# Two weight lines of a pair of banks: highs of both, then lows of both, in a pinned order

## The chip, the cores and the metric

The kernel runs on one core of a Trainium2 chip. The metric is the time of one execution on the device, in microseconds (us); before the change the median of three runs is 1748.11 us (1747.93 to 1748.73).

The engines are named as in the profile: PE is TensorE's matmuls and PEld its weight loads, DVE is VectorE, ACT is ScalarE, POOL is GpSimd, SP is SyncE.

## What is computed

A trunk of two layers on 256 tokens of width 1024, all in float32. Layer 0 mixes tokens by a gated short convolution, layer 1 by windowed attention. After each comes a channel mixer, PEER, that looks up experts by product keys. All norms are RMS norms. Cut to what matters here:

```
gate_b, gate_c, h = split(x @ w_in, 3)          # 1024 -> 3 x 1024, layer 0
x = x + (gate_b * conv(gate_c * h)) @ w_out
...
q  = t @ w_q                                    # 1024 -> 2048
idx, g = top 16 experts of 16384 by the keys, for each of 8 heads
h  = einsum("cd,ced->ce", t, u_tab[idx])        # chosen rows of u
x  = x + einsum("ce,ced->cd", g * gelu(h), v_tab[idx])
```

The kernel does not gather the expert rows. It multiplies the tokens by all 16384 rows of u, and by all of v with gates that are zero where an expert was not chosen.

## The kernel before

**Lines and their halves.** Every weight matrix is cut into lines of 128 x 1024 float32 (512 KB). `split_tile` (L176 to L185) loads a line into `raw` (four buffers) on SyncE's queue. ScalarE rounds it to `hi` (three buffers, L183), VectorE subtracts to get `lo` (two buffers, L184). The activation `xn` holds, for each of 8 blocks of 128 inputs, 256 columns of high halves and beside them 256 of low halves. A product of a line is high weights by high and by low activations, and low weights by high activations.

**Two forms of a product.** `wide_product` (L248) gives a line a bank of 512 columns: 8 matmuls of `hi` by all 512 columns (high and low activations side by side), then 8 of `lo` by the first 256. `sum_of_parts` (L259) later copies the right half of both banks (ScalarE) and adds the left half (VectorE). `cols_product` (L220), the narrow form, sums everything in 256 columns, with 24 matmuls. Its order depends on its last argument; without one it is 8 of `lo`, then 16 of `hi`:

```
turns = [(lo, k, 0) for k in range(KC)] + [(hi, k, n) for k in range(KC) for n in range(2)]
```

**Which lines are wide.** In `conv_mixer` (loop at L471) each j takes three lines: two that share a pair of banks, wide for j = 1 to 6, and one for the gate, always narrow (L484). In `peer`, stage pq (L989) takes 16 lines two by two, all wide but the first two. Stage ph, over u, takes 128 lines in two halves of 64, two by two (L1106):

```
wide = (j % 4 == 2 or j >= HALF // 2) if half == 0 else j < HALF - 2
```

So wide and narrow pairs alternate in the first 32 lines, and the last pair of all is narrow. Stage pv, over v, has products of 512 columns of another kind (`rows_product`), which the change leaves alone.

**Order of the work.** `take()` (L208) first brings the queue of split lines to two, then takes the first; so the line after the one in hand is split while that one is multiplied. A new `lo` waits until the matmuls of the line two before have read theirs. Which instruction stands where in its engine's queue is settled at compile time by a scheduler that follows program order and the readiness that it reckons with; an edge (`tc.issue_after(ins)`) keeps an instruction behind another on its engine. `bg.pump()` (L56) is called between products and hands out pieces of background work, mostly VectorE's: top 16 of the scores, gates, one-hot tables (L1025) and their small products pg on TensorE (L1040). Each piece is kept behind the latest `lo` on VectorE.

**Banks.** Wide pairs have two pairs of banks in turn (`two_banks`, L137), narrow products one bank each.

Of the kernel before, what the change touches and what calls it, by code (L numbers as in the profile page):

```python
# [18 lines left out]
T = 256  # L19
D = 1024  # L20
NT = T // P
KC = D // P
# [53 lines left out]
def trunk_kernel(  # L76
# [29 lines left out]
    bg = Background(tc)  # L106

    newest = []

    def matmul(*a, **k):  # L110
        newest[:] = [PE.matmul(*a, **k).ins]  # L111
        return newest[0]
# [5 lines left out]
    def in_turn():  # L118

        return tc.issue_after(newest[0])  # L120
# [11 lines left out]
    def bank(tag, name):  # L132
        if tag == "acc":
            return four_banks(False).tile([P, 512], F32, tag=tag, name=name, bufs=4)
        return ps.tile([P, 512], F32, tag=tag, name=name, bufs=2)
# [40 lines left out]
    def split_tile(src, spare=False, pieces=1):  # L176
        raw = strm.tile([P, D], F32, tag="raw", name="raw", bufs=4)
        hi = strm.tile([P, D], F32R, tag="hi", name="hi", bufs=3)
        lo = strm.tile([P, D], F32R, tag="oh2" if spare else "lo", name="lo", bufs=2)
        n = D // pieces  # L180
        for c in (slice(n * i, n * i + n) for i in range(pieces)):
            nc.sync.dma_start(raw[:, c], src[:, c])
            bg.rounded = S.copy(hi[:, c], raw[:, c]).ins  # L183
            bg.behind = V.tensor_tensor(lo[:, c], raw[:, c], hi[:, c].bitcast(F32), ALU.subtract).ins  # L184
        return hi, lo  # L185
# [22 lines left out]
    def take(n=2):  # L208

        prefetch(n)  # L210
        return ahead.popleft()

    def prefetch(n, spare=False, pieces=1):
        while order and len(ahead) < n:
            with ExitStack() as held:
                for ins in evicted:
                    held.enter_context(tc.issue_after(ins))
                ahead.append(split_tile(order.popleft(), spare, pieces))

    def cols_product(dst, w, act, nth=None):  # L220

        hi, lo = (a.rearrange("p (k c) -> p k c", k=KC) for a in w)
        if nth == 0:
            turns = [(w, k, n) for w, n in ((hi, 0), (lo, 0), (hi, 1)) for k in range(KC)]
        elif nth == 1:
            turns = [(w, k, n) for w, n in ((hi, 0), (hi, 1), (lo, 0)) for k in range(KC)]
        else:
            turns = [(lo, k, 0) for k in range(KC)] + [(hi, k, n) for k in range(KC) for n in range(2)]
        for i, (w, k, n) in enumerate(turns):
            matmul(dst, w[:, k], act[:, k, T * n : T * n + T], start=(i == 0), stop=(i == 3 * KC - 1))  # L230
# [14 lines left out]
        run([turn for k in range(4, KC) for turn in ((hi, k - 4, 1), (hi, k, 0), (lo, k, 0))])  # L245
        run([(hi, k, 1) for k in range(4, KC)], stop=True)

    def wide_product(b, w, act, between=None):  # L248

        hi, lo = (a.rearrange("p (k c) -> p k c", k=KC) for a in w)  # L250
        for k in range(KC):
            matmul(b, hi[:, k], act[:, k], start=(k == 0), stop=False)
        if between:
            with in_turn():
                between()
        for k in range(KC):
            matmul(b[:, :T], lo[:, k], act[:, k, :T], start=False, stop=(k == KC - 1))

    def sum_of_parts(dst, b):  # L259
        S.copy(dst, b[:, :, T:])  # L260
# [149 lines left out]
    def factors():  # L410

        b = bank("g", "pyb")
        for t in range(NT):
            transpose(b[:, P * t : P * t + P], stat[:, 8 + t : 9 + t].to_broadcast([P, P]), ident)
        S.copy(yb, b[:, :T])
# [29 lines left out]
    def conv_mixer(sc):  # L445
        cw = sc(KC, 3)
        xn = turned_x(0, big.tile([P, KC, 2 * T], F32R, tag="xa", name="xn"))
        wait_for(nc.gpsimd.dma_start(cw, conv_w).ins, [bg.rounded])
        loaded = load_buckets(sc)
        z = big.tile([P, KC, 2 * T], F32R, tag="HB", name="z")  # L450
        ring = [(sc(2, T), sc(T + 2), sc(T)) for _ in range(2)]
        for _, ch, _ in ring:
            V.memset(ch, 0.0)

        def mixed(j, b0, b1):
            cs, ch, y = ring[j % 2]
            if 0 < j < KC - 1:
                sum_of_parts(cs, b0)
                V.tensor_tensor(cs, cs, yb[:, None, :].to_broadcast([P, 2, T]), ALU.mult)
            else:  # L460
                times_factor(cs, b0, 2)
            V.tensor_tensor(ch[:, 1 : T + 1], cs[:, 0], cs[:, 1], ALU.mult)
            V.tensor_scalar(y, ch[:, 0:T], cw[:, j, 0:1], None, op0=ALU.mult)
            V.scalar_tensor_tensor(y, ch[:, 1 : T + 1], cw[:, j, 1:2], y, op0=ALU.mult, op1=ALU.add)
            V.scalar_tensor_tensor(y, ch[:, 2 : T + 2], cw[:, j, 2:3], y, op0=ALU.mult, op1=ALU.add)
            V.tensor_tensor(y, y, yb, ALU.mult)
            V.tensor_tensor(y, b1[:, :T], y, ALU.mult)
            S.copy(z[:, j, :T], y)
            V.tensor_tensor(z[:, j, T:], y, z[:, j, :T].bitcast(F32), ALU.subtract)

        for j in range(KC):  # L471
            if j == 2:
                bias_rows(*loaded)
                blank_table(1)
            wide = 0 < j < KC - 1
            b0, b1 = two_banks("pconv") if wide else bank("u", "pconv"), None
            for i in range(2):
                if wide:
                    between = (lambda: (factors(), mixed(*left))) if (j, i) == (1, 0) else None
                    wide_product(b0[:, i], take(), xn, between)  # L480
                else:
                    cols_product(b0[:, T * i : T * i + T], take(), xn, 3 * j + i)
            b1 = bank("g", "pgate")
            cols_product(b1[:, :T], take(), xn)  # L484
            if j == 0:
                left = j, b0, b1
            else:
                mixed(j, b0, b1)
        acc = accumulators("pout")
        for k in range(KC - 2):  # L490
            rows_product(acc, take(), z[:, k, :T], z[:, k, T:], k == 0)
        return last_rows(acc, [(take(KC - k), z[:, k, :T], z[:, k, T:]) for k in (KC - 2, KC - 1)])
# [250 lines left out]
    def peer(layer, last, meanwhile):  # L743
# [8 lines left out]
        xr = turned_x(1 + 2 * layer, big.tile([P, KC, 2 * T], F32R, tag="HA", name=f"xr{layer}"), last, bq[:, :T])  # L752
        xn = big.tile([P, KC, 2 * T], F32R, tag="xa", name="xn")
# [235 lines left out]
        for c in range(0, NSUB, 2):  # L989
            q = qT[(c // 4) % 2][:, c % 4 : c % 4 + 2]  # L990
            b = two_banks("pq") if c else bq
            for i in range(2):
                if c:
                    wide_product(b[:, i], take(), xr)
                elif i:
                    cols_product(b[:, T:], take(), xr, i)
                bg.pump()
            if c:
                sum_of_parts(q, b)
            else:  # L1000
                S.copy(q, b.rearrange("p (a t) -> p a t", a=2))
            if c == 2:
                factors()
            if c >= 4 and c % 4 == 0:
                compared(c - 4)
# [91 lines left out]
        for half, hm in enumerate(halves):  # L1097
            if half == 1:
                spread_half(0)
                bg.plan(bg.cost(), HALF - 4)  # L1100
            for j in range(0, HALF, 2):
                if half == 0 and j == HALF // 2:
                    bg.drain()
                    second_tile()
                    bg.plan(bg.cost(), HALF // 2 + 14)
                wide = (j % 4 == 2 or j >= HALF // 2) if half == 0 else j < HALF - 2  # L1106
                b = two_banks("ph") if wide else bank("u", "ph")
                for i in range(2):
                    if wide:
                        wide_product(b[:, i], take(), xn)  # L1110
                    else:
                        cols_product(b[:, T * i : T * i + T], take(), xn)
                    bg.pump()
                if wide:
                    sum_of_parts(hm[:, j : j + 2], b)
                    S.activation(hm[:, j : j + 2], hm[:, j : j + 2], AF.Gelu)  # L1116
                else:
                    S.activation(hm[:, j : j + 2], b.rearrange("p (a t) -> p a t", a=2), AF.Gelu)
                if half == 0 and j == 0:
                    first_picks()  # L1120
                if half == 1 and j >= HALF - 16 and j % 4 == 0:
                    far_pump()
# [70 lines left out]
        for j in range(0, P, 2):  # L1193
# [12 lines left out]
            a = aring[:, (j // 2) % 4]  # L1206
# [44 lines left out]
    total, part, root = stat[:, 4:6], stat[:, 6:8], stat[:, 8:10]  # L1251
# [34 lines left out]
    for n, (t, c) in enumerate(ends):  # L1286
        h = c.start // 512
        if c.start == 768:
            b = bank("u", "pend")[:, :T]
# [99 lines left out]
```

## Time and profile before

| | |
|---|---|
| median of three runs | 1748.11 us |
| the profiled execution | 1748.41 us |
| its span, first to last instruction | 1746.6 us |
| VectorE busy | 1358.3 us, 78% |
| ScalarE busy | 931.7 us, 53% |
| one rounding to `hi` (L183) | 1049 ns, 595 times |
| one subtraction to `lo` (L184) | 1221 ns, 595 times |
| moved by DMA | 375.51 MB, 215 GB/s on average |

The timeline lists start, duration, engine, line, operation and count, with successive instructions of one kind merged. Matmuls overlap: one of 512 columns lasts some 393 ns, and the next starts 227 ns after it; so the pace is read from starts. Line 111 is the helper through which every matmul goes, and tiles are told apart by name: pconv and pgate (convolution), pq, ph, pv and pg (PEER).

### The profile page before, as it was taken

How to read it: one execution, taken by the hardware profiler on the slowest of the kernel's cores; microseconds unless marked ns; L12 is line 12 of the kernel's file. 1: busy time of each engine (PE TensorE's matmuls, PEld its weight loads, DVE VectorE, ACT ScalarE, POOL GpSimd, SP SyncE). 2: the span in 40 equal slices, each digit the busy share in tenths (PEclk: the TensorE clock that was granted, in tenths of full speed). 3: DMA queues.
4: the chain of work that ended last, by engine and by line, in shares of the span. 5: the costliest groups of instructions: out<-in, count | busy, mean ns of one | idle time of the engine just before them, and what ended most of it. 6: DMA issues, size and time to landing. Idle time of an engine off the chain costs nothing.

```text
span 1746.6 us, 28965 instructions
## 1 busy us (share of the span) xinstructions
PE 1736.7 (99%) x10153; PEld 1503.1 (86%) x10153; DVE 1358.3 (78%) x2850; ACT 931.7 (53%) x1262; POOL 1026.2 (59%) x584
## 2 busy tenths in 40 slices
PE   9999999999999999999999999999999999999998
PEld 7989998888888888888888899888888888888886
DVE  7869989987777667666586899898877777666765
ACT  5455555565545444454476655655655544444544
POOL 1112888888888886530010148888888888865100
PEclk9999999999999999999999999999999999999999
DMA  7987777776679898998685867777766798988884
GB/s 258 313 279 222 185 182 192 188 187 182 169 177 238 220 221 235 272 267 242 213 274 171 285 176 190 183 192 187 189 176 174 190 234 221 222 239 232 245 241 136
DMA packets 255698, 375.51 MB, mean 215 GB/s; under 512 B 135765, under 2 KB 170613, under 8 KB 255296
## 3 DMA queue, kind: packets, MB, share of 16 engines
q1 hardware_dynamic: 86976, 314.35, 55.9%
q0 software_dynamic: 82112, 30.69, 16.3%
q10 hardware_dynamic: 86464, 28.62, 6.7%
q8 instruction: 79, 1.29, 0.3%
q14 instruction: 67, 0.55, 0.1%
HBM read 344.96 MB, written 28.61 MB: 214 GB/s over the span
## 4 chain that ended last, share of the span: by engine, by line
PE 98%; DVE 1%; ACT 0%; issue 0%; DVEq 0%; ACTq 0%
PE ph L111 41%; PE pv L111 40%; PE pq L111 6%; PE pconv L111 3%; PE pgate L111 1%; PE psc L111 1%; PE pwo L111 1%; PE pg L111 1%; PE pout L111 1%; PE po L111 0%; PE ppt L115 0%; PE pk L111 0%; DVE xs L300 0%; PE ptr L115 0%; PE pwarm L111 0%; ACT xn L344 0%
## 5 line engine op out<-in xcount | busy, mean ns | idle before, releaser
L183 ACT CAST hi<-raw 128x1024 fp32r<-128x1024 f32 (+1 forms) x597 | 625.2, 1048 | 588.4 <-PE pv L111 192.8
L184 DVE TENSOR_TENSOR lo<-raw,hi 128x1024 fp32r<-128x1024 f32 (+1 forms) x597 | 726.1, 1219 | 271.6 <-ACT hi L183 152.0
L539 POOL DMA_INDIRECT table<-route x256 | 473.5, 1850 | 129.6 <-issue 74.4
L111 PE MATMUL ph<-xn,hi 128*128 128x512 f32 (+1 forms) x2336 | 515.3, 366 | 0.1
L111 PE MATMUL pv<-hi,xn 128*128 128x512 f32 (+1 forms) x2048 | 507.9, 389 | 0.0
L111 PEld LDWEIGHTS pv<-hi,xn 128*128 128x128 f32 x2048 | 384.2, 188 | 79.7
L539 POOL DMA_INDIRECT far_table<-yb x192 | 366.4, 1908 | 119.0 <-DMA far_table<-yb 59.8
L111 PEld LDWEIGHTS ph<-xn,hi 128*128 128x128 f32 x2336 | 387.0, 190 | 56.9 <-DVE route L261 0.2
L111 PEld LDWEIGHTS ph<-xn,lo 128*128 128x128 f32 x2048 | 275.8, 191 | 17.4 <-DVE lo L184 0.4
L111 PE MATMUL ph<-xn,lo 128*128 128x256 f32 x2048 | 283.5, 282 | 0.0
L111 PE MATMUL pv<-lo,xn 128*128 128x512 f32 x1024 | 277.0, 390 | 0.0
L111 PEld LDWEIGHTS pv<-lo,xn 128*128 128x128 f32 x1024 | 191.5, 188 | 39.3 <-DVE lo L184 0.3
L539 POOL DMA_INDIRECT set_table<-yb x64 | 134.7, 2104 | 19.5 <-issue 19.2
L1162 POOL DMA_DIRECT2D far_gates<-far_table x28 | 15.3, 546 | 150.6 <-DVE route L1175 126.5
L527 POOL DMA_DIRECT2D table<-blank x16 | 18.6, 1165 | 138.8 <-DMA table<-blank 96.1
L1181 ACT CAST xn<-hm 128x512 fp32r<-128x512 f32 x64 | 39.9, 623 | 74.9 <-PE pv L111 73.8
L1182 DVE TENSOR_TENSOR xn<-hm,xn 128x512 fp32r<-128x512 f32 x64 | 44.2, 691 | 35.8 <-ACT xn L1181 27.8
L111 PE MATMUL pq<-xr,hi 128*128 128x512 f32 (+1 forms) x288 | 68.2, 374 | 0.2
L1181 ACT CAST xn<-route 128x512 fp32r<-128x512 f32 x64 | 39.7, 620 | 46.8 <-PE pv L111 45.7
L1182 DVE TENSOR_TENSOR xn<-route,xn 128x512 fp32r<-128x512 f32 x64 | 44.0, 688 | 24.3 <-ACT xn L1181 23.7
L111 PEld LDWEIGHTS pq<-xr,hi 128*128 128x128 f32 x288 | 49.5, 189 | 8.9 <-ACT xr L344 0.8
L1116 ACT ACTIVATE route<-route 128x512 f32<-128x512 f32 x62 | 39.0, 629 | 15.2 <-DVE oh L1036 7.8
(216 smaller groups left out, 1478.9 us busy)
## 6 DMA issues: line engine op xcount, KB each, us to landing
raw<-in_u SPq DMA_DIRECT2D x256, 512.0 KB
raw<-in_v SPq DMA_DIRECT2D x256, 512.0 KB
table<-blank POOLq DMA_DIRECT2D x16, 1024.0 KB
raw<-in_w_q SPq DMA_DIRECT2D x32, 512.0 KB
gates<-table ACTq DMA_DIRECT2D x128, 128.0 KB
raw<-in_w_in SPq DMA_DIRECT2D x23, 512.0 KB
far_table<-blank POOLq DMA_DIRECT2D x6, 1024.0 KB
raw<-in_w_qk SPq DMA_DIRECT2D x10, 512.0 KB
```

What stands on the lines that cost most here:

```text
L111: newest[:] = [PE.matmul(*a, **k).ins]
L183: bg.rounded = S.copy(hi[:, c], raw[:, c]).ins
L184: bg.behind = V.tensor_tensor(lo[:, c], raw[:, c], hi[:, c].bitcast(F32), ALU.subtract).ins
L527: ins = nc.gpsimd.dma_start(dst, blank[:, None, :].to_broadcast([P, ROWS // P, P])).ins
L539: nc.gpsimd.indirect_dma_start(to, bass.IndirectOffsetOnAxis(ap=places[:, c : c + 1], axis=0), gates[:, c : c + 1], None, compute_op=ALU.a ...
L1116: S.activation(hm[:, j : j + 2], hm[:, j : j + 2], AF.Gelu)
L1162: ins = (nc.gpsimd if i == 2 else nc.scalar).dma_start(f[:, i], part).ins
L1181: copied[:] = [S.copy(a[:, 0], src).ins]
L1182: return V.tensor_tensor(a[:, 1], src, a[:, 0].bitcast(F32), ALU.subtract).ins
```

## The change

`wide_product` becomes `wide_pair`, which takes both lines of a pair first and multiplies high of the first, high of the second, low of the first, low of the second. Background work is handed out after the second part and after the last. The split of the next line is asked for after the first line's lows, that of the line behind it after the second line's. Each matmul of these pairs, and the narrow products of conv_mixer, pq and ph as groups, are kept behind the one before by an edge, so the order of products on TensorE is that of the program.

```diff
-    def wide_product(b, w, act, between=None):
-
-        hi, lo = (a.rearrange("p (k c) -> p k c", k=KC) for a in w)
-        for k in range(KC):
-            matmul(b, hi[:, k], act[:, k], start=(k == 0), stop=False)
+    chain = []
+
+    def after_chain():
+        return tc.issue_after(chain[0]) if chain else ExitStack()
+
+    def narrow(dst, act, nth=None):
+        with after_chain():
+            cols_product(dst, take(), act, nth)
+        chain[:] = newest
+
+    def wide_pair(b, act, between=None):
+
+        pair = [[a.rearrange("p (k c) -> p k c", k=KC) for a in take(2 - i)] for i in range(2)]
+
+        def part(i, low):
+            for k in range(KC):
+                with after_chain():
+                    chain[:] = [
+                        matmul(b[:, i, :T], pair[i][1][:, k], act[:, k, :T], start=False, stop=(k == KC - 1))
+                        if low else matmul(b[:, i], pair[i][0][:, k], act[:, k], start=(k == 0), stop=False)
+                    ]
+
+        part(0, False)
         if between:
             with in_turn():
                 between()
-        for k in range(KC):
-            matmul(b[:, :T], lo[:, k], act[:, k, :T], start=False, stop=(k == KC - 1))
+        part(1, False)
+        bg.pump()
+        part(0, True)
+        prefetch(1)
+        part(1, True)
+        prefetch(2)
+        bg.pump()
...
-            for i in range(2):
-                if wide:
-                    between = (lambda: (factors(), mixed(*left))) if (j, i) == (1, 0) else None
-                    wide_product(b0[:, i], take(), xn, between)
-                else:
-                    cols_product(b0[:, T * i : T * i + T], take(), xn, 3 * j + i)
+            if wide:
+                wide_pair(b0, xn, (lambda: (factors(), mixed(*left))) if j == 1 else None)
+            else:
+                for i in range(2):
+                    narrow(b0[:, T * i : T * i + T], xn, 3 * j + i)
             b1 = bank("g", "pgate")
-            cols_product(b1[:, :T], take(), xn)
+            narrow(b1[:, :T], xn)
...
-                for i in range(2):
-                    if wide:
-                        wide_product(b[:, i], take(), xn)
-                    else:
-                        cols_product(b[:, T * i : T * i + T], take(), xn)
-                    bg.pump()
+                if wide:
+                    wide_pair(b, xn)
+                else:
+                    for i in range(2):
+                        narrow(b[:, T * i : T * i + T], xn)
+                        bg.pump()
```

The loop of pq is changed in the same way as that of ph.

More of the change, by code (lines that the diff above doesn't have):

```diff
@@ L991, in peer @@
             b = two_banks("pq") if c else bq
-            for i in range(2):
[L993 to L996, printed above, removed]
+            if c:
+                wide_pair(b, xr)
+            else:
+                bg.pump()
+                narrow(b[:, T:], xr, 1)
                 bg.pump()
@@ L1107, in peer @@
                 b = two_banks("ph") if wide else bank("u", "ph")
-                for i in range(2):
-                    if wide:
-                        wide_product(b[:, i], take(), xn)
-                    else:
-                        cols_product(b[:, T * i : T * i + T], take(), xn)
-                    bg.pump()
+                if wide:
+                    wide_pair(b, xn)
+                else:
+                    for i in range(2):
+                        narrow(b[:, T * i : T * i + T], xn)
+                        bg.pump()
                 if wide:
```

## The prediction

> **What bounds the kernel now.** I read the busy times of the page first, then the chain that ended last, then what the weight loads of TensorE wait for, then the groups by shape, and at last the timeline, in a quiet stretch and around one change of form.
>
> ```profile
> span 1746.6 us, 28965 instructions
> ...
> PE 1736.7 (99%) x10153; PEld 1503.1 (86%) x10153; DVE 1358.3 (78%) x2850; ACT 931.7 (53%) x1262; POOL 1026.2 (59%) x584
> ...
> PEclk9999999999999999999999999999999999999999
> ...
> PE 98%; DVE 1%; ACT 0%; issue 0%; DVEq 0%; ACTq 0%
> ```
>
> TensorE is busy for 99% of the span, holds 98% of the chain and has its clock throughout. Whatever TensorE waits is added to the time, and whatever other engines wait is not. The waits of the weight loads say how well the split of the weights keeps up:
>
> ```profile
> PEld ph L111 <- DVE lo L184: 0.4, 1, 0.4
> PEld pv L111 <- DVE lo L184: 0.3, 1, 0.3
> ```
>
> In 1746.6 us the loads waited twice for a low half from VectorE. So VectorE is not late today; the question is by how much.
>
> Now the shapes, with the columns line, engine, operation, tile, shape and count, then busy us and mean ns:
>
> ```profile
> L111 PE MATMUL ph<-xn,hi 128*128 128x512 f32 x1760 | 442.6, 393 | 0.1
> ...
> L111 PE MATMUL pq<-xr,hi 128*128 128x512 f32 x224 | 56.8, 395 | 0.0
> ...
> L111 PE MATMUL ph<-xn,hi 128*128 128x256 f32 x576 | 75.0, 283 | 0.0
> ...
> L111 PE MATMUL pconv<-xn,hi 128*128 128x512 f32 x96 | 24.3, 393 | 0.0
> ```
>
> A wide line has 8 high products of 512 columns, a narrow one 16 of 256. So there are 1760/16 = 110 wide pairs in ph, 224/16 = 14 in pq and 96/16 = 6 in pconv: 130 pairs. The 576 high products of 256 columns are 36 narrow lines of ph.
>
> **What the new order gains on TensorE.** Start times, not durations, give the pace, since the matmuls overlap. A quiet stretch of ph (start us, us, engine, line, operation, count):
>
> ```profile
> 350.08 1.12 PE L111 MATMUL ph<-xn,lo 128*128 128x256 f32 x8
> 351.03 2.00 PE L111 MATMUL ph<-xn,hi 128*128 128x512 f32 x8
> 352.87 1.11 PE L111 MATMUL ph<-xn,lo 128*128 128x256 f32 x8
> 353.82 2.00 PE L111 MATMUL ph<-xn,hi 128*128 128x512 f32 x8
> 355.66 1.12 PE L111 MATMUL ph<-xn,lo 128*128 128x256 f32 x8
> ```
>
> And a stretch of pv, where every product has 512 columns:
>
> ```profile
> 535.20 1.07 PE L111 MATMUL pv<-lo,xn 128*128 128x512 f32 x4
> 536.11 1.98 PE L111 MATMUL pv<-hi,xn 128*128 128x512 f32 x8
> 537.92 1.07 PE L111 MATMUL pv<-lo,xn 128*128 128x512 f32 x4
> ```
>
> In pv twelve products take 537.92 - 535.20 = 2.72 us, 0.227 each. In ph eight highs take 351.03 to 352.87, 1.84 us, where eight at the pace of pv would take 1.81: a run of 512 columns that follows one of 256 loses 0.03 us at its start. Eight lows take 0.95 us, and sixteen in a row (178.64 to 180.56 in the next fence) 1.92, so a run of lows gains 0.01 where it follows highs. One return trip from highs to lows and back costs 0.02 us. The change removes one trip of two from each of 130 pairs: 130 x 0.02 = 2.6 us gained. The bounds are nothing and twice that, since starts are given to 0.01 us and the difference is two such steps.
>
> The Trainium skill ("TensorE: Matmul & The Clock Gate", Back-to-back issue gap) gives the gap between matmuls by their columns alone, N / 2.4 + 2.5 ns, which leaves no cost to the change from 256 to 512 columns; by that the reordering itself would gain 0. The trace does not agree: the 512-column runs differ by 0.03 us with what stands before them.
>
> **What it costs: the low half of the next narrow line.** Low halves lie in two buffers. Today the first line's lows are multiplied before the second line's highs, so its buffer is free 2.79 us (351.03 to 353.82) before the pair ends. After the change both low buffers are held until the pair's last quarter. If a wide pair follows, that is no matter: it begins with highs, of which there are three buffers. A narrow line without its own order begins with its lows. The trace around such a change of form, a wide pair whose second line is followed by a narrow line:
>
> ```profile
> 175.85 1.12 PE L111 MATMUL ph<-xn,lo 128*128 128x256 f32 x8
> 176.80 2.00 PE L111 MATMUL ph<-xn,hi 128*128 128x512 f32 x8
> 178.64 2.08 PE L111 MATMUL ph<-xn,lo 128*128 128x256 f32 x16
> 180.56 2.08 PE L111 MATMUL ph<-xn,hi 128*128 128x256 f32 x16
> ```
>
> ```profile
> 177.06 1.22 DVE L184 TENSOR_TENSOR lo<-raw,hi 128x1024 fp32r<-128x1024 f32 x1 [0.30 <-issue]
> ```
>
> ```profile
> 180.44 1.99 PEld L111 LDWEIGHTS ph<-xn,hi 128*128 128x128 f32 x16
> ```
>
> The x16 of lows is the second line's eight and the narrow line's eight. The low half of the narrow line is written by the VectorE row: it starts at 177.06, 0.09 us after the first line's lows end (175.85 + 1.12 = 176.97), which is when their buffer comes free, and is ready at 178.28. Its first load comes eight lows after 178.64, near 179.5: a slack of some 1.2 us, all of it from the second line's highs that lie between.
>
> The change takes just those highs away from between. Count from the start of the first line's lows: VectorE starts at 177.06 - 175.85 = 1.21 and is done at 2.43. How long from there to the load is shown where TensorE did wait, at the first narrow line of ph behind pq:
>
> ```profile
> 153.75 1.22 DVE L184 TENSOR_TENSOR lo<-raw,hi 128x1024 fp32r<-128x1024 f32 x1
> ```
>
> ```profile
> 155.02 1.01 PEld L111 LDWEIGHTS ph<-xn,lo 128*128 128x128 f32 x8
> ```
>
> The load starts 155.02 - 154.97 = 0.05 us after the write ends. So the narrow line can start at 2.48. TensorE is there earlier: sixteen lows of the pair take 1.92 us, and a load goes 0.12 us ahead of its matmul (180.44 against 180.56), so it asks at 1.80. It waits 2.48 - 1.80 = 0.68 us, with nothing of the pinned chain to put in between: pinned, the narrow line's highs stand behind its lows.
>
> How often: the loops give it. In ph's first half lines 4, 8, ..., 28 are narrow and follow a wide pair (7), in the second half the last pair is narrow (1), and ph's first narrow line follows pq's last wide pair (1): 9 a layer, 18. In conv_mixer the gate's line follows the wide pair for j = 1 to 6: 6. Together 24 x 0.68 = 16.3 us. The second narrow line is not late: its low half is written right after, done at 2.43 + 1.22 = 3.65, and asked for a whole narrow line (24 products at 0.12 = 2.88) after 2.48.
>
> Bounds for one wait: nothing below 0.6 follows from these rows, as the write itself (1.22) outlasts the second line's lows (0.95). Upward it grows if VectorE is busy when the buffer comes free. The write at 153.75 is such a case today, since its load had to wait; but there VectorE will have 1.84 us more before the buffer is free, as long as the background steps keep their place, so I take 0.68 for all and put the rest into the range.
>
> **What moves at no cost.** Highs have three buffers and are wanted a full line earlier than lows; two of three stay as they are, and the third comes free earlier, after the pair's first highs. A load into raw is issued when a low half is done, today one every 2.79 us, afterwards two 1.22 us apart every 5.58 us. Of the waits of ScalarE's casts these stand side by side (us, times, longest):
>
> ```profile
> ACT hi L183 <- PE ph L111: 191.6, 147, 2.8
> ...
> ACT hi L183 <- DMA raw<-in_u: 20.6, 11, 3.4
> ```
>
> The cast waits for a buffer 147 times and for the transfer 11 times, and no load of ph waits for it, so four raw buffers cover the bunching; if they did not, a wide pair would be late by what the transfer lacks. SyncE's queue holds only such loads. VectorE's low halves for the next wide pair are ready at 2.43 and 3.65 on the same count and are wanted at 1.92 + 16 x 0.227 + 0.03 - 0.12 = 5.46 and 0.96 later: slacks of 2.98 and 2.77 us. The two background calls of a pair now both lie between the second low half and the next pair's first. The evacuation still follows the pair's last low, as the two banks were summed together before too.
>
> **The sum.** The profiled execution took 1748.41 us, 1.8 above its span and 0.3 above the median of 1748.11. 1748.4 + 16.3 - 2.6 = 1762.1, with the median's 0.3 off 1761.8: I say 1762.
>
> **The rivals.** *Grouping without the wait.* If the narrow line's lows were ready (a free buffer, or VectorE far ahead), only the gain is left: 1748.1 - 2.6 = 1745.5, faster. It needs fewer than 2.6 / 0.68 = 4 waits of the 24. Two buffers speak against it, and the 0.09 us between their release and the write. Chance 0.07.
>
> *The change does not do what it says*: TensorE follows the old order anyway, or the pair is broken up by other work. Then 1748, no change. The chain of products is explicit, so 0.05.
>
> *VectorE's blocks become the bound for wide pairs too.* In ph's second half the one-hot steps come in one block between two low halves:
>
> ```profile
> 449.51 1.23 DVE L184 TENSOR_TENSOR lo<-raw,hi 128x1024 fp32r<-128x1024 f32 x1 [0.91 <-PE ph L111]
> 450.65 0.69 DVE L1033 TENSOR_TENSOR oh<-iota,i1T 128x1024 bf16<-128x1024 bf16 x1
> ...
> 455.33 1.08 DVE L1038 TENSOR_TENSOR oh<-oh,gT 128x512 bf16<-128x512 bf16 x3
> 456.33 2.35 DVE L184 TENSOR_TENSOR lo<-raw,hi 128x1024 fp32r<-128x1024 f32 x2
> ```
>
> From 450.74 to 456.33 is 5.59 us. After the change the free gap between pairs of low halves is 5.58 - 2 x 1.22 = 3.14, so the block makes the next two 2.45 late, and of the slack of 2.77 for the second 0.3 is left. A block longer by 0.3, or one caught between the two low halves, stalls TensorE. There are 16 one-hot steps a layer, done two by two: 16 blocks in all. If each costs 0.7 us, that is 11 us more: 1773. It decides from the point where a block exceeds 5.9 us. Chance 0.18.
>
> *Only the wait, no gain*: each product costs what its own columns cost, whatever stands before it, and 1748.1 + 16.3 = 1764.4. The 0.03 us by which runs of highs differ speak against it: 0.06. It is what the formula of the Trainium skill cited above ("TensorE: Matmul & The Clock Gate", Back-to-back issue gap) would make of the change.
>
> **How the numbers follow.** The forecast, the wait less the gain, has 0.64: 1762, by itself 1757 to 1768 (half to twice the gain, and waits 0.3 us longer in a third of the places, or absent in a quarter). The range takes in the blocks and the case without gain, and reaches down to where half the waits are gone: 1753 to 1774. Left out are the faster case and no change, 0.12, and blocks dearer than 0.7 us. A measurement of this kernel can tell 0.2% (3.5 us) from no change. Slower by more: 0.64 + 0.18 + 0.06 = 0.88; within 0.2%: 0.05 for no change and 0.03 of the case without the wait, whose 2.6 us lie inside 0.2%, together 0.08; faster by more: the other 0.04 of that case, where the gain is nearer its upper bound.
>
> **What would show it.** Right: the waits of PEld have a new line for ph behind lo of L184 with about 18 entries of 0.6 to 0.8 us, and one for pgate with 6; the timeline has x16 highs of 512 columns and lows behind them; each VectorE write of a narrow line's low half starts 0.1 us after the pair's first lows end. The busy share of TensorE falls by about 1 in 100. Wrong: no such waits (then the buffer was free, and the time falls), or waits at wide pairs in ph's second half (then the blocks), or waits behind hi of L183 or a raw transfer, which none of the steps above has.

## The result and the profile after

| | before | after |
|---|---|---|
| median of five runs | 1748.04 us (1747.68 to 1748.73) | 1765.37 us (1764.84 to 1766.95) |
| the profiled execution | 1748.41 us | 1764.84 us |
| its span | 1746.6 us | 1763.1 us |

The ratio is 1.01, 95% interval 1.0088 to 1.0111: the change makes the kernel 17.3 us slower. The forecast was 1762, so it was short by 3.4 us, inside its range. In the three longer of the five runs after (1765.37 to 1766.95) the mean granted clock of TensorE is 0.998, in the other two (1764.84, which was profiled, and 1764.98) it is 0.999, as before the change.

The page of the kernel after, in the order in which it was read before: span, busy times, chain.

```profile
span 1763.1 us, 28971 instructions
...
PE 1739.3 (99%) x10153; PEld 1502.7 (85%) x10153; DVE 1349.3 (77%) x2850; ACT 941.1 (53%) x1262; POOL 1004.9 (57%) x584
...
PE 91%; DVE 5%; issue 2%; DMA 1%; ACT 1%; SPq 0%; ACTq 0%; DVEq 0%
```

The busy share of TensorE is 99% in both, and hides the loss twice. It is rounded: 1746.6 - 1736.7 = 9.9 us were idle before, 1763.1 - 1739.3 = 23.8 us are idle after. And matmuls overlap, so a late one leaves a gap that is shorter than its delay. The chain says it better: TensorE's share falls from 98% to 91%, and VectorE's rises to 5%. (5% of the span is 88 us, far more than was lost, since the chain runs on through whole VectorE steps whenever TensorE waits for one's end.) The waits of the weight loads (us, times, longest):

```profile
PEld ph L111 <- DVE lo L184: 13.4, 17, 2.3
...
PEld pgate L111 <- DVE lo L184: 3.5, 5, 1.0
...
PEld pgate L111 <- ACT mix L283: 1.0, 1, 1.0
```

Behind `lo` of L184 there was one entry of 0.4 for ph before; there are 17 now, and 5 for pgate. The entry put down to `mix` is the sixth gate: VectorE's write came after the mixing there too. The timeline around a change of form in ph, a wide pair followed by a narrow line (the convention is that of the prediction: start, duration, engine, line):

```profile
184.63 2.07 PE L111 MATMUL ph<-xn,lo 128*128 128x256 f32 x16
...
185.84 2.36 DVE L184 TENSOR_TENSOR lo<-raw,hi 128x1024 fp32r<-128x1024 f32 x2 [1.43 <-issue]
...
187.12 1.01 PEld L111 LDWEIGHTS ph<-xn,lo 128*128 128x128 f32 x8 [0.62 <-DVE lo L184]
187.12 1.22 PE L111 MATMUL ph<-xn,lo 128*128 128x256 f32 x8 [0.42 <-DVE lo L184]
```

The x16 is the pair's lows of both lines. VectorE starts 185.84 - 184.63 = 1.21 us after them, the narrow line's first load comes at 187.12, 2.49 after. Without a wait it would come at 1.80 (1.92 for sixteen lows less the lead of 0.12): 0.69 us lost. Three readings of one delay stand in these rows: 0.62 is idle time of the loads, counted from the end of the load before, which normally overlaps the next; 0.42 is the gap in the overlapping matmuls; 0.69 is what the end of the kernel sees. The entries of the waits add up so: 2.28 + 1.80 behind pq (below) and 15 of some 0.62 (0.56 to 0.68) make 13.4.

Where the time came from, by stage, each counted from its first weight load to that of the next, in us:

| stage | before | after | difference |
|---|---|---|---|
| start | 10.34 | 9.89 | -0.45 |
| pconv, pgate | 69.58 | 74.10 | +4.52 |
| pq, layer 0 | 51.88 | 54.52 | +2.64 |
| ph, layer 0 | 371.88 | 375.91 | +4.03 |
| pq, layer 1 | 51.79 | 54.05 | +2.26 |
| ph, layer 1 | 372.12 | 375.78 | +3.66 |
| all others | 819.03 | 818.80 | -0.23 |

All of the loss lies in the stages that have wide pairs. In pq the loss is at its end, where ph's first narrow line waits:

```profile
157.15 2.08 PE L111 MATMUL pq<-xr,lo 128*128 128x256 f32 x16
...
159.02 0.18 DVE L844 TENSOR_SCALAR route<-route 128x32 uint32<-128x32 uint32 x1
...
160.38 0.19 DVE L853 TENSOR_TENSOR route<-route 128x32 bf16<-128x32 f32 x1
160.50 2.35 DVE L184 TENSOR_TENSOR lo<-raw,hi 128x1024 fp32r<-128x1024 f32 x2
161.77 1.01 PEld L111 LDWEIGHTS ph<-xn,lo 128*128 128x128 f32 x8 [2.28 <-DVE lo L184]
```

The buffer is free 1.21 us after 157.15, at 158.36. VectorE writes into it only at 160.50: until then it works through routing steps that the background calls handed out ahead of the write. In layer 1 the same place waits 1.80. One of the two dear gates looks alike, with mixing steps in the place of routing:

```profile
51.46 2.07 PE L111 MATMUL pconv<-xn,lo 128*128 128x256 f32 x16
...
52.75 0.43 DVE L492 TENSOR_TENSOR z<-mix,z 128x256 fp32r<-128x256 f32 x1 [0.47 <-ACT z L491]
53.10 2.35 DVE L184 TENSOR_TENSOR lo<-raw,hi 128x1024 fp32r<-128x1024 f32 x2
54.37 1.01 PEld L111 LDWEIGHTS pgate<-xn,lo 128*128 128x128 f32 x8 [1.04 <-DVE lo L184]
```

The write starts 1.64 us after the lows instead of 1.21. By starts of matmuls, 0.1 us added for the slower second one, the six gates lose 1.04, 0.68, 0.73, 1.10, 0.62 and 0.62: 4.8 us together. The sum of all waits: 16 changes of form in ph, 14 at 0.68 (one of them 0.74) and two at 0.62 where a layer ends (10.8), two behind pq (2.36 + 1.88 = 4.2), six gates (4.8): 19.8 us, against 16.3 in the forecast.

### The profile page after: what moved, and what is told of

It reads as the page before. It is cut to its first block, busy times and chain, and to the rows that moved or that the text cites. A ratio compares the mean times of both kernels' runs of the same rounds, so it can differ in the third digit from the quotient of the medians.

```text
span 1763.1 us, 28971 instructions
## 1 busy us (share of the span) xinstructions
PE 1739.3 (99%) x10153; PEld 1502.7 (85%) x10153; DVE 1349.3 (77%) x2850; ACT 941.1 (53%) x1262; POOL 1004.9 (57%) x584
## 3 DMA queue, kind: packets, MB, share of 16 engines
q8 instruction: 79, 1.29, 0.3%
## 4 chain that ended last, share of the span: by engine, by line
PE 91%; DVE 5%; issue 2%; DMA 1%; ACT 1%; SPq 0%; ACTq 0%; DVEq 0%
PE pv L111 40%; PE ph L111 38%; PE pq L111 4%; DVE lo L184 2%; PE pconv L111 2%; PE pwo L111 1%; PE pout L111 1%; PE pg L111 1%; PE pgate L111 1%; PE psc L111 1%; ACT hi L183 1%; PE po L111 0%; DMA raw<-in_w_in 0%; PE ppt L115 0%; DMA raw<-in_w_q 0%
## 5 line engine op out<-in xcount | busy, mean ns | idle before, releaser
L184 DVE TENSOR_TENSOR lo<-raw,hi 128x1024 fp32r<-128x1024 f32 (+1 forms) x597 | 718.6, 1221 | 264.6 <-ACT hi L183 146.7
L561 POOL DMA_INDIRECT table<-route x256 | 455.1, 1778 | 135.7 <-issue 74.4
L111 PE MATMUL ph<-xn,hi 128*128 128x512 f32 (+1 forms) x2336 | 493.3, 364 | 0.1
L111 PEld LDWEIGHTS ph<-xn,hi 128*128 128x128 f32 x2336 | 394.1, 189 | 63.0 <-DVE route L284 0.3
L561 POOL DMA_INDIRECT far_table<-yb x192 | 378.3, 1970 | 114.3 <-DMA far_table<-yb 57.4
L111 PE MATMUL ph<-xn,lo 128*128 128x256 f32 x2048 | 271.6, 284 | 10.4 <-DVE lo L184 9.9
L111 PEld LDWEIGHTS ph<-xn,lo 128*128 128x128 f32 x2048 | 261.5, 191 | 21.6 <-DVE lo L184 13.4
L561 POOL DMA_INDIRECT set_table<-yb x64 | 119.8, 1872 | 24.1 <-issue 18.9
```

The costliest lines, as they stand in the source:

```text
L561: nc.gpsimd.indirect_dma_start(to, bass.IndirectOffsetOnAxis(ap=places[:, c : c + 1], axis=0), gates[:, c : c + 1], None, compute_op=ALU.a ...
```

## The experiments

Theory: narrow lines begin with lows, and their low half cannot be written before the pair's last quarter, since both low buffers are held; TensorE waits 0.68 us at 24 places, more where VectorE is busy, and the order of wide pairs itself gains some 0.02 us a pair. Rivals: the edges that pin the order cost the time; or the order of products inside wide pairs does, whatever follows them; or products cost by their columns alone, and nothing is gained. Every experiment is an edit of the kernel after unless said. "Before" in a result is the kernel before on the same chip.

**Narrow lines begin with highs** (e1), and the same edit made in the kernel before (e4).

```diff
-            cols_product(dst, take(), act, nth)
+            cols_product(dst, take(), act, 1 if nth is None else nth)
```

> The changed kernel, in which every narrow line of conv_mixer and ph that had its lows first now has its 16 highs first and its lows last. If the loss is the wait for the narrow line's low half (0.68 us, 24 times, more behind pq), sixteen highs at 0.12 us are 1.92 us of work ahead of the lows and cover it: the waits of PEld for lo of L184 in ph and pgate go, and the time falls below the old kernel's by the gain of the grouping, 1745 to 1746 us. If the loss is the pinned order by itself, or VectorE's load, it stays near 1765.

Measured: 1749.33 us, before 1747.95; ratio 1.0006 (0.9997 to 1.0015). Of the 17.3 us 16 are gone with the lows' turn alone, while highs of both lines still stand ahead of lows and the order is pinned. ph takes 371.61 and 371.55 us, 0.3 and 0.6 less than before. So the loss sits at the narrow lines, not in the wide pairs. The time expected was 1745 to 1746, below the kernel before by the gain of the grouping, and that was missed by 3 to 4 us: waits use the gain up. The largest lie in pconv, which takes 72.22, 2.6 more than before. From the trace of this kernel, in that stage:

```profile
66.20 1.22 DVE L184 TENSOR_TENSOR lo<-raw,hi 128x1024 fp32r<-128x1024 f32 x1
67.33 0.42 DVE L485 TENSOR_TENSOR mix<-mix 128x256 f32<-128x256 f32 x1
...
70.28 0.42 DVE L490 TENSOR_TENSOR mix<-pgate,mix 128x256 f32<-128x256 f32 x1
70.62 1.22 DVE L184 TENSOR_TENSOR lo<-raw,hi 128x1024 fp32r<-128x1024 f32 x1
...
71.89 1.00 PEld L111 LDWEIGHTS pgate<-xn,lo 128*128 128x128 f32 x8 [1.38 <-DVE lo L184]
```

Six mixing steps, from 67.33 to 70.70, stand between the pair's second low half and the gate's, which comes later than the gate's own highs can cover. Matmuls wait 1.34 us here and 0.26, 0.40 and 0.42 at three other places; with 0.1 each for the slower second product that is 2.8. In conv_mixer the mixing leaves VectorE too little room. Behind pq, in ph's first narrow line, the loads still wait 0.65 and 0.55 us for its low half, 1.3 with the slower second products. So 4.1 us of waits stand against a gain of 2.6 (the pairs of ph repeat every 5.567 us here too, see the account below). That is read from the trace; no run isolates it.

> The old kernel with only the narrow lines' order turned, highs first: the control for the same turn in the changed kernel. The old one has no waits there to win back, and the number of changes between 512 and 256 columns is the same, so both theories expect no change, 1747.5 to 1748.5 us. If it were faster by itself, that would have to be taken off what the turn does in the changed kernel. The difference to the changed kernel with highs first is the gain of the grouping alone, 2.6 us by the forecast (130 pairs at 0.02).

Measured: 1748.77 us, before 1747.95; 1.0004 (0.9995 to 1.0013). In the old order the turn of the narrow lines makes no difference. It matters only behind grouped pairs.

**Three highs first, then the lows** (e2): a dose between the two, 3 x 0.12 = 0.36 us of cover.

```diff
+        elif nth == 3.5:
+            turns = [(hi, k, 0) for k in range(3)] + [(lo, k, 0) for k in range(KC)]
+            turns += [(hi, k, 0) for k in range(3, KC)] + [(hi, k, 1) for k in range(KC)]
...
-            cols_product(dst, take(), act, nth)
+            cols_product(dst, take(), act, 3.5 if nth is None else nth)
```

> The changed kernel with three of the narrow line's highs (256 columns) ahead of its eight lows in conv_mixer and ph, the other thirteen behind. A dose: three highs are 0.36 us of the 0.68 us that the line waits for its lows. If the wait is what the buffer and VectorE's write make it, each of the 24 waits falls by 0.36 us: 1765.4 - 8.6 = 1756.8 us, with waits of 0.32 us left in ph. If the waits came from the order of VectorE's queue, they would move with it and the time stay near 1765.

Measured: 1758.18 us, before 1748.2; 1.0062 (1.0048 to 1.0076). The waits of this kernel's loads:

```profile
PEld ph L111 <- DVE lo L184: 7.1, 18, 1.9
PEld pgate L111 <- DVE lo L184: 3.0, 6, 0.9
```

Without the two behind pq (1.85 and 1.14) the 16 others have (7.1 - 3.0) / 16 = 0.26 of idle loads, where the kernel after has 0.62: the 0.36 of cover came off one for one. Of the 1.4 us above the expectation 0.7 lie at the gates (pconv is 72.68 us, 1.42 under the kernel after, where six times 0.36 would be 2.16) and 0.6 in the start (10.48).

**The pins alone, and the order alone.** e5 keeps the edges and puts the old order back; e3 keeps the order of the program and drops the edges.

```diff
         part(0, False)
...
-        part(1, False)
-        bg.pump()
         part(0, True)
+        bg.pump()
         prefetch(1)
+        part(1, False)
         part(1, True)
```

> The changed kernel with its pins, but each pair in the old order: high and low of the first line, then high and low of the second; the split of the next line is asked for after the first line's lows. If the loss is the buffer that the grouping holds longer, the waits go and the time is the old one's, 1747 to 1749 us. If pinning costs by itself, it stays above that, up to 1765.

Measured: 1748.89 us, before 1747.95; 1.0006 (0.9997 to 1.0015). Pinning the old order costs nothing that can be measured.

```diff
     def after_chain():
-        return tc.issue_after(chain[0]) if chain else ExitStack()
+        return ExitStack()
```

> The changed kernel without the edges that pin the order of products; all else as it is. The order that the scheduler then writes puts two or three highs of 512 columns of a later pair (0.227 us each) ahead of most narrow lines' lows. If the loss is the wait of 0.68 us, these fill 0.45 us of it some 20 times: 1765.4 - 9 = about 1756 us, with waits of 0.2 us left. If the grouping itself costs (more distance between highs and lows), it stays at 1765; if the pin is all of the loss, it comes to 1746 to 1748.

Measured: 1759.26 us, before 1747.95; 1.0066 (1.0053 to 1.008): 6.1 us under the kernel after by the medians, 3 over the expectation. A change of form in this kernel:

```profile
183.54 2.08 PE L111 MATMUL ph<-xn,lo 128*128 128x256 f32 x16
185.45 0.63 PE L111 MATMUL ph<-xn,hi 128*128 128x512 f32 x2
186.03 1.22 PE L111 MATMUL ph<-xn,lo 128*128 128x256 f32 x8
```

The narrow line's lows start 186.03 - 183.54 = 2.49 us after the pair's, to the hundredth as in the kernel after: the low half is no earlier. But two products of a later wide pair have been put ahead of them, and these fill 2 x 0.227 = 0.45 of the 0.68. The trace has such a pair at 14 places of ph, 6.3 us. So pins keep the scheduler from filling a wait that another part of the change makes. The expectation was too low for two reasons. Behind pq (loads idle for 1.80 and 2.10 us) and at the gates the scheduler filled little. And right after the second of these waits, which ends at 1026.01, the granted clock is 0.50 from 1027.5 to 1030.9 us: products of 256 columns start 0.213 us apart there instead of 0.120, which costs 3.4 x (1 - 0.120/0.213) = 1.5 us. The mean granted clock is 0.998 in all five runs of this kernel.

**A third low buffer** (e7). To make room, `raw` goes from four buffers to three; e10 has that price alone.

```diff
-name="lo", bufs=2)
+name="lo", bufs=2 if spare else 3)
...
-name="raw", bufs=4)
+name="raw", bufs=3)
```

> The changed kernel with three buffers for low halves, paid for by one of the four buffers for raw lines (there is no room for both). The narrow line's low half need then not wait for the pair's lows. If the wait is for the buffer, it goes, and the time is 1745 to 1748 us, more by whatever three raw buffers cost, which would show as waits of ScalarE's casts and PEld for raw and hi. If VectorE's queue is the cause, the waits behind lo of L184 stay and the time is 1765 or more.

Measured: 1756.27 us, before 1748.2; 1.0046 (1.0032 to 1.006). A change of form, and what the loads wait for:

```profile
180.96 3.04 PE L111 MATMUL ph<-xn,lo 128*128 128x256 f32 x24
183.83 2.08 PE L111 MATMUL ph<-xn,hi 128*128 128x256 f32 x16
```

```profile
PEld pyb L115 <- DVE stat L347: 3.4, 3, 2.0
...
PEld ph L111 <- DVE lo L184: 0.6, 1, 0.6
```

24 lows stand in a row without a gap, the pair's sixteen and the narrow line's eight. ph takes 371.90 and 370.84 us (375.91 and 375.78 after). What is left of the loss lies elsewhere: in attention above all, 90.68 us instead of 86.36, and in pconv, 71.83 instead of 69.58 before, where the loads of two gates still wait 1.7 us together for `lo`.

> The changed kernel with three buffers for raw lines instead of four and still two for low halves: the control for the run with three low buffers. If the third low buffer is what took the waits behind lo of L184 away in ph, they are back here (24 waits, some 18 us of idle), and the time is that run's 1756.3 and about 16 us more, 1772, as the price of three raw buffers outside ph stays. If the three raw buffers themselves had shifted the queues so that the waits went, they stay away and the time is near 1756.

Measured: 1794.58 us, before 1748.12; 1.0255 (1.0241 to 1.0269). The expectation missed by 22 us. The waits of the loads:

```profile
PEld ph L111 <- DVE lo L184: 17.0, 18, 3.7
PEld pgate L111 <- DVE lo L184: 8.1, 5, 3.7
PEld ph L111 <- ACT hi L183: 5.0, 10, 1.0
```

All waits behind `lo` are back, with two low buffers, and new ones behind `hi`, which ph of the kernel after has not. So it is the third low buffer that removed them in e7. Most of the miss is the price of the fewer raw buffers. The casts of ScalarE wait for a transfer of u 176 times here, 119 times in e7 and 80 times in the kernel after: a raw buffer is held until its low half is written, so with two low buffers that are held longer, three raws leave the transfers too late, and with three low buffers they do much less.

Part of the miss is the clock. Behind the wait of 3.44 us at pq's end in layer 1, products of 256 columns start like this:

```profile
1052.47 3.62 PE L111 MATMUL ph<-xn,hi 128*128 128x256 f32 x16
1055.88 1.34 PE L111 MATMUL ph<-xn,lo 128*128 128x256 f32 x8
```

Sixteen take 1055.88 - 1052.47 = 3.41 us, 0.213 each instead of 0.120. The granted clock of this profile is 0.50 in four stretches ahead of the kernel's end (from 49.4, 80.2 and 172.3 us for 3.4 us each, from 1049.5 for 6.8), and each begins in a wait of the loads of 2.2 to 3.7 us or at most 0.5 us behind one. TensorE works in 15.8 of these 17.1 us and loses 15.8 x (1 - 0.120/0.213) = 6.9 to the clock. Over the five runs, too, the time goes with it: 1788.88 us at a mean clock of 0.997, 1791.5 at 0.995, 1794.58 to 1795.94 at 0.993 and 0.994.

**Where the background stands behind pq** (e6). Only for pq's last pair, the first of the two background calls goes behind the request for the narrow line's split.

```diff
...
         part(1, False)
-        bg.pump()
+        if early:
+            bg.pump()
         part(0, True)
         prefetch(1)
         part(1, True)
         prefetch(2)
+        if not early:
+            bg.pump()
         bg.pump()
...
-                wide_pair(b, xr)
+                wide_pair(b, xr, None, c < NSUB - 2)
```

> The changed kernel with one background call moved: in the last pair of pq the first of the two calls comes behind the pair, so that routing steps handed out there stand behind the low half of ph's first narrow line on VectorE. If the two longest waits (about 2.3 and 1.8 us, at the change from pq to ph) are VectorE working through routing steps that the change put ahead of that low half, they fall to 0.7 us each: 1765.4 - 2.7 = 1762.7 us. If they have another cause (the small products of pq's scores, a late transfer), nothing changes.

Measured: 1762.18 us, before 1748.2; 1.0079 (1.0066 to 1.0093).

```profile
157.78 2.08 PE L111 MATMUL pq<-xr,lo 128*128 128x256 f32 x16
158.93 2.36 DVE L184 TENSOR_TENSOR lo<-raw,hi 128x1024 fp32r<-128x1024 f32 x2 [0.35 <-PE pq L111]
...
160.21 1.02 PEld L111 LDWEIGHTS ph<-xn,lo 128*128 128x128 f32 x8
...
171.08 2.07 PE L111 MATMUL ph<-xn,lo 128*128 128x256 f32 x16
172.94 2.39 DVE L184 TENSOR_TENSOR lo<-raw,hi 128x1024 fp32r<-128x1024 f32 x2
174.24 1.02 PEld L111 LDWEIGHTS ph<-xn,lo 128*128 128x128 f32 x8 [1.29 <-DVE lo L184]
```

Now VectorE itself waits for the buffer, writes 1.15 us after the lows begin, and four small products of the scores fill what is left. The waits of 2.28 and 1.80 us are gone. Some 1.2 us come back at the next change of form, where the postponed steps now stand (in layer 0 the write starts 1.86 after the lows, and the wait is 1.29 where 0.62 is usual; in layer 1 it is 1.20 where 0.68 stood). By stages pq is 3.8 us shorter and ph 1.05 longer, together 2.8: the expected 2.7, but otherwise divided than expected (two waits of 0.7 left behind pq), so the near hit is in part luck. This shows that the long waits behind pq came from background work queued ahead of the write.

**The price of a trip** (e9). The order is line after line, pinned, and each wide line goes through 4 highs, 4 lows, 4 highs, 4 lows: one return trip more for each of the 260 wide lines.

```diff
-        def part(i, low):
-            for k in range(KC):
+        def part(i, low, k0=0, k1=KC):
+            for k in range(k0, k1):
...
-        part(0, False)
-        if between:
-            with in_turn():
-                between()
-        part(1, False)
-        bg.pump()
-        part(0, True)
-        prefetch(1)
-        part(1, True)
+        for i in range(2):
+            for k in (0, KC // 2):
+                part(i, False, k, k + KC // 2)
...
+                part(i, True, k, k + KC // 2)
+            if not i:
+                bg.pump()
+                prefetch(1)
```

> The pinned kernel with the old line after line, but each wide line in two halves: four highs, four lows, four highs, four lows. A pair then makes four trips between 512 and 256 columns instead of the old kernel's two (and the changed kernel's one), with the same products. If a trip costs 0.017 to 0.02 us, two more in each of 130 pairs cost 4.4 to 5.2 us: 1752.5 to 1753.5. If a product costs what its columns cost, whatever stands before it, the time is that of the pinned old order, 1748 to 1749.

Measured: 1752.19 us, before 1748.12; 1.0024 (1.0015 to 1.0033).

```profile
333.45 1.09 PE L111 MATMUL ph<-xn,hi 128*128 128x512 f32 x4
334.38 0.64 PE L111 MATMUL ph<-xn,lo 128*128 128x256 f32 x4
334.86 1.09 PE L111 MATMUL ph<-xn,hi 128*128 128x512 f32 x4
```

Four highs take 0.93 us, where 4 x 0.227 = 0.91. The 4.07 us above the kernel before are 0.016 a trip (0.010 to 0.022 by the interval), a little less than the 0.017 expected at least. Against e5, which has the same pins, ph is longer by 1.71 and 1.63 us for 110 trips each: 0.015. Some 0.4 us of that are two new waits for low halves (0.40 and 0.33 of idle loads); in undisturbed stretches a pair of ph repeats every 5.613 us here and every 5.587 in e5, which is 0.013 a trip. This is the price of a trip between runs of four products; that of the change, between runs of eight or sixteen, is read in the account below and is larger. The Trainium skill ("TensorE: Matmul & The Clock Gate", Back-to-back issue gap) has gaps that depend on columns alone, which would make e9 as fast as e5; the measurement decides against it, by a small amount.

**Grouped only where a wide pair follows** (e8): 104 of the 130 pairs, the old order elsewhere, all pinned. It keeps the gain and has no narrow line behind a grouped pair.

```diff
...
+        if grouped:
             part(1, False)
             bg.pump()
             part(0, True)
             prefetch(1)
+        else:
+            part(0, True)
+            bg.pump()
+            prefetch(1)
+            part(1, False)
         part(1, True)
...
```

> The changed kernel with a pair grouped only where a wide pair follows it (46 pairs of ph and 6 of pq in each layer, 104 in all) and in the old order where a narrow line follows (all of conv_mixer, pq's last pair, ph's first 32 lines and its last wide pair); all pinned. If the loss sits only where a narrow line follows, all 24 waits go and the gain of the grouping is left: 104 x 0.017 to 0.02 us = 1.8 to 2.1 us, so about 1746 us. If grouping delays VectorE's work in ph's second half too, it stays above 1748.

Measured: 1747.69 us, before 1748.2; 0.9997 (0.9988 to 1.0006). The waits of 0.6 us and more are gone. The low half of a narrow line is still late at two places of ph, one a layer:

```profile
201.62 1.02 PEld L111 LDWEIGHTS ph<-xn,lo 128*128 128x128 f32 x8 [0.19 <-DVE lo L184]
```

The other is at 1062.80, and e5 has the same two (0.19 and 0.20), so they do not come from the grouping. ph takes 371.27 and 371.29, 0.6 and 0.8 less than before. (The profiled execution, 1745.86, was the fastest of the eleven.) The median misses the expected 1746 by 1.7. The loss is gone, and by the times alone what is left of the gain can't be told from nothing. No kernel of this study is measurably faster than the one before.

## Why the prediction was nearly right, point by point

- **What bounds the kernel**: right. Every stage that grew did so by waits of TensorE, and all that lies behind the start and has no wide pairs kept its length within 0.3 us.
- **The gain**: right. In a quiet stretch of the kernel after ten pairs of ph take 358.75 - 303.08 = 55.67 us, in the same stretch of the kernel before 358.46 - 302.59 = 55.87:

```profile
303.08 3.82 PE L111 MATMUL ph<-xn,hi 128*128 128x512 f32 x16
...
358.75 3.82 PE L111 MATMUL ph<-xn,hi 128*128 128x512 f32 x16
```

```profile
302.59 1.12 PE L111 MATMUL ph<-xn,lo 128*128 128x256 f32 x8
...
358.46 1.12 PE L111 MATMUL ph<-xn,lo 128*128 128x256 f32 x8
```

  A pair takes 5.567 us instead of 5.587, so a trip is worth 0.020 and 130 pairs gain 2.6 us. The forecast had this from two differences of 0.03 and 0.01 between starts that are given to 0.01 us, and allowed for nothing to twice that; that it hit the third decimal is luck. The rival "only the wait, no gain" is refuted by this, and by e9 in its premise.
- **One wait**: right. 0.69 measured for 0.68 at the ordinary places of ph; VectorE's start at 1.21 and the load at 2.49 are the forecast's 1.21 and 2.48. The row that its 0.05 us from write to load was read from was a weak one (the load came late there, but its matmul kept its pace); the rows after bear it out, with the first write's end at 185.84 + 1.22 = 187.06 and the load at 187.12. e1, e2 and e7 (with e10 as its control) show the cause: it shrinks by the cover put ahead of the lows and goes with a third buffer.
- **How often**: right, 18 in ph (the list of waits has 17 behind `lo`; the eighteenth, at 211.12 us, has the same 0.62 and is put down to issue) and 6 gates.
- **The term that was mis-sized**: "there VectorE will have 1.84 us more before the buffer is free, as long as the background steps keep their place, so I take 0.68 for all". They do not keep their place. The edit moves a background call between the second line's highs and the first line's lows, so its steps stand ahead of the low half that the narrow line wants. The prediction says so itself ("The two background calls of a pair now both lie between the second low half and the next pair's first"), but drew from it only what it means for a wide pair that follows. Behind pq this made 2.36 and 1.88 us where 1.36 together was allowed: 2.9 us more; e6 shows it. Two gates behind mixing steps add 0.7 (4.8 in place of 4.1). The start, 0.45 us shorter in the profile, and the stages without wide pairs, 0.2 shorter, go the other way. That is 2.9 us, where the two spans differ by 16.4 instead of 13.7, 2.7 more. The medians give 3.4; that three of the five runs after have a mean clock of 0.998 would fit stretches of half clock behind the long waits, as e3's trace has one, but no trace shows those runs.
- **The bounds**: "1757 to 1768" does not follow from the conditions given with it. Half the gain and eight waits longer by 0.3 make 1765.7, twice the gain and a quarter of the waits absent 1755.3. The measured 1765.37 lies inside both.
- **No cost at the highs and the raw loads**: right for the kernel as it is, with no wait of ph behind `hi`. That four raw buffers cover the bunching was near the edge: ScalarE's casts wait for a transfer of u 80 times after, 11 times before, and e10 shows what the fourth is worth.
- **VectorE's blocks as a bound for wide pairs**: did not happen. One such stretch of the kernel after:

```profile
461.98 0.69 DVE L1055 TENSOR_TENSOR oh<-iota,i1T 128x1024 bf16<-128x1024 bf16 x1 [2.64 <-PE pg L111]
...
465.13 2.35 DVE L184 TENSOR_TENSOR lo<-raw,hi 128x1024 fp32r<-128x1024 f32 x2
```

```profile
467.35 2.09 PEld L111 LDWEIGHTS ph<-xn,lo 128*128 128x128 f32 x16
```

  The first of the two low halves is done at 465.13 + 1.22 = 466.35, 1.0 us ahead of the first load. The smallest slack of a wide line anywhere in ph is 0.71; the forecast had feared 0.3. (Its slacks of 2.98 and 2.77 are on two counts: with the 0.05 from write to load taken off both, the second is 2.72.)
- **What would show it**: the waits came as named. The busy share of TensorE as a sign was poor: it falls from 99.4% to 98.7%, and the page shows 99% for both.

## What to carry to other kernels

When an order holds a buffer longer, ask what follows at each place where the form of the work changes: the loss is not in the reordered part but in the first consumer behind it that needs the freed buffer at once. Then look at what else the edit moves on the producing engine's queue, background calls included, since a step queued ahead of the write adds its whole length to the wait. An order may be pinned without cost while nothing waits, but a pinned order also keeps every wait that the scheduler would have filled. And look at the granted clock behind the longest waits before a difference is put down to the waits alone.

## What was not expected of the hardware

- A run of 512-column products behind 256-column ones starts slowly and settles: gaps between starts of 233, 236, 228, 232, 231, then 226 to 227 ns, in the traces of this case. Less what the first low behind highs gains (113 instead of 120 ns) that is the 0.020 us of a trip; in runs of four it is 0.013.
- A wait can cost twice. In e3 the clock falls to half for 3.4 us, 1.5 us after the end of a wait of 2.10 us, and in e10 four times, in or right behind waits of 2.2 to 3.7. It need not come: the profile of the kernel after has a wait of 2.28 us and no such stretch before the kernel's end.
- One raw buffer fewer costs 29 us in the kernel after (e10 against 1765.37, on another chip), some 7 of them by the clock, while e7, which has that and a third low buffer, is 9 us faster than the kernel after. Rings that feed one another can't be priced one at a time.
